# The gates of an RG-LRU in a fused decoder block: six 128-feature matmuls per step, or four by blocks of 64 features with the high and low parts stacked

## The chip, the cores and the metric

The kernel runs on one core of a Trainium2 chip. Its engines work side by side, each with its own instruction stream: TensorE (PE) multiplies matrices into PSUM, VectorE (DVE) and ScalarE (ACT) do elementwise work, GpSimd (POOL) does some as well, and DMAs, most of them issued by SyncE (SP), move data between HBM and the on-chip SBUF. The metric is the device time of one execution in microseconds. Before the change the median of three runs is 2132.93 us (2130.52 to 2132.96). The profiled execution took 2130.19 us, of which 2128.4 us lie between its first and its last instruction (the span).

## The reference

One layer of a decoder block over 2048 positions and 1024 features: a combined input projection to 9216 columns, a dilated-window attention branch, a gated linear recurrence (RG-LRU) branch, a merge, an output projection and a layer norm. The change concerns the recurrence's gates alone:

```python
def rg_lru(x, w_r, b_r, w_i, b_i, lam):
    xb = x.reshape(B, S, LRU_BLOCKS, LRU_BLOCK_WIDTH)          # 16 blocks of 64
    r = sigmoid(einsum('bsgi,gij->bsgj', xb, w_r).reshape(B, S, C) + b_r)
    i = sigmoid(einsum('bsgi,gij->bsgj', xb, w_i).reshape(B, S, C) + b_i)
    log_a = -LRU_C * r * softplus(-lam)
    a = exp(log_a)
    u = sqrt(maximum(-expm1(2.0 * log_a), 0.0)) * (i * x)
    # h_t = a_t * h_(t-1) + u_t, an associative scan over the positions
```

Here x is the output of a width-4 causal convolution. The gate weights are block-diagonal: a feature reaches only the 64 features of its own block.

## The kernel before

**Precision.** Every fp32 product is made from parts. A value is copied to a rounded type (fp32r) as its high part, and the rest, the value minus that, is its low part. A product of two such values takes three matmuls: high times high, high times low, low times high.

**Stages.** The projection comes first and takes until about 1453 us of the span. It computes 72 column tiles of 128 features over four chunks of 512 positions, by a Strassen-like scheme: two column tiles and two chunks at a time, seven products instead of eight. There are two halves (chunks 0 and 1, then 2 and 3) of 36 such units each, and each product has 12 matmuls of 128 rows by 512 columns into one of four PSUM banks (tag `q`). Attention follows, and then the merge, the output projection and the layer norm.

**Ticks and queues.** The program is put into order while it is built. A product is a tick, 506 of them (L902 to L920). In each tick come, in this order, the product's matmuls, the events fixed for this tick, the work put off with `later`, the chains, and the evacuation of the product's bank. Each engine's instructions run in the order of their emission, so an instruction that waits holds up all that stand behind it on its engine.

**Events** load and prepare the weights. `load_w` (L224) has SP load a block of weights (the tiles `wA` and `wS` of the profile), three to six ticks ahead of the unit's preparation. `sums` (L239) has DVE form the sums `S` of blocks, `prep_w` (L259) has ACT make the high part (`hA`, `hS`, L264) and DVE the low part (`l`). In the first half the low parts go to HBM (`wl_scr`), in the second half they are read back (`load_lo`, L279).

**Chains** are generators that work on from a finished tile. A chain asks (`Ask`) for free slots, a number of ticks to pass and a share of each engine's time in a tick (`LEN`, 2.75 us); what it asks for is taken from the tick's budget, and it goes on when budget, slots and conditions allow. `ALONE` scales DVE's share in the first half.

**The recurrence chain** `lru(i, c, ub)` (L427) handles feature tile i (128 features, two blocks) and chunk c, 32 chains in all; tiles 0, 2, 4 and 6 put chunk 1 off to the second half. In sixteen of them (`bring_gw`) the gate weights come first: two DMAs on SP into `gr` (L438, L439), each 128 rows of 128 numbers from the block-diagonal matrices that the layout built. Then follow the convolution into `v` (ACT L447, DVE L449), the high and the low part of the weights into `gw` (ACT L456, DVE), the high and the low part of v (`vh`, ACT L463; `vl`, DVE), the gate matmuls in the middle of the next product (L472 to L474, put there by `pe_later`), the two tanh that leave PSUM (ACT L485 for r, L486 for i, with the halved biases `brh`), the exponentials, the square root and the scan (L507). At most two such chains are live at a time, and `gate["busy"]` keeps one gate step at a time in the two PSUM banks of tag `g`.

**At the start** ACT issues the DMAs of the biases and the recurrence's vectors (L73, L78) before anything else; `consts` (L851) scales them once the first product has been emitted.

Of the kernel before, what the change touches and what calls it, by code (L numbers as in the profile page):

```python
# [8 lines left out]
F32 = mybir.dt.float32  # L9
F32R = mybir.dt.float32r  # L10
AF = mybir.ActivationFunctionType
ALU = mybir.AluOpType
# [19 lines left out]
def hybrid_block_kernel(ctx: ExitStack, tc: tile.TileContext, a: dict, out: bass.AP):  # L32
# [3 lines left out]
    def flat(t):  # L36
        return t.bitcast(F32)
# [39 lines left out]
    lr = cst.tile([P, 8, 8], F32, name="lr")  # L77
    act.dma_start(lr, a["lru_vec"])  # L78
    brh = cst.tile([P, 2, 8], F32, name="brh")
    sp2 = cst.tile([P, 8], F32, name="sp2")  # L80


# [47 lines left out]
    def take(name, dt=F32R):  # L130
        if not vacant:
            raise RuntimeError(f"no slot at {now['n']}: {[x[1].name if hasattr(x[1],'name') else x[1] for x in home.values()]} chains {len(chains)}")
        i = vacant.pop(0)
        t = sl_p.tile([P, CH], dt, tag=f"s{i}", name=name)
        home[id(t)] = (i, t)
        return t
# [81 lines left out]
    def tt(eng, out, in0, in1, op):  # L218
        eng.tensor_tensor(out=out, in0=in0, in1=in1, op=op)  # L219
# [207 lines left out]
    def lru(i, c, ub):  # L427
# [7 lines left out]
        if bring_gw:  # L435
            yield Ask(lag=0, need=1, keep=1)
            gr = take("gr" + nm, F32)
            sp.dma_start(gr[:, 0:P], a["wr"][i])  # L438
            sp.dma_start(gr[:, P:2 * P], a["wi"][i])  # L439
        if c == 1 and i in put_off:  # L440
            yield Ask(lag=4)
        yield Ask(lag=0, need=1, keep=6, cond=lambda: gate["live"] < 2 and begun[i] == c, ACT=1.3, DVE=2.7)
# [14 lines left out]
            tt(dve, w[:, 2 * P:], gr[:, 0:2 * P], flat(w[:, 0:2 * P]), ALU.subtract)  # L457
            give(gr)
        yield Ask(lag=0, cond=lambda: gated[i] == c)
        gw = GW[i].rearrange("p (l j f) -> p l j f", l=2, j=2)  # L460
        yield Ask(need=2, keep=1, ACT=.66, DVE=.75)
        vh, vl = take("vh" + nm), take("vl" + nm)
        act.activation(vh, v, AF.Copy)  # L463
        tt(dve, vl, v, flat(vh), ALU.subtract)
        yield Ask(lag=2, cond=lambda: not gate["busy"])
        gate["busy"] = True
        pg = []

        def gates():
            for j in range(2):  # L470
                g = ps.tile([P, CH], F32, tag="g", name=f"g{j}{nm}", bufs=2)
                pe.matmul(g, gw[:, 0, j], vh, start=True, stop=False)  # L472
                pe.matmul(g, gw[:, 0, j], vl, start=False, stop=False)
                pe.matmul(g, gw[:, 1, j], vh, start=False, stop=True)  # L474
                pg.append(g)
            give(vh, vl)
            if c in ((0, 3) if i in put_off else (1, 3)):
                give(GW[i])

        pe_later(1, gates)  # L480
        gated[i] = c + 1
        yield Ask(lag=2, need=3, keep=1, ACT=3.3, DVE=.75)
        gate["busy"] = False
        tr, ti, e = take("tr" + nm, F32), take("ti" + nm, F32), take("e" + nm, F32)
        act.activation(tr, pg[0], AF.Tanh, scale=0.5, bias=brh[:, 0, i:i + 1])  # L485
        act.activation(ti, pg[1], AF.Tanh, scale=0.5, bias=brh[:, 1, i:i + 1])  # L486
        act.activation(e, tr, AF.Exp, scale=sp2n[:, i:i + 1], bias=sp2n[:, i:i + 1])
        act.activation(e, e, AF.Identity, scale=0.5, bias=half_t)
        act.activation(tr, tr, AF.Tanh, scale=sp2[:, i:i + 1], bias=sp2[:, i:i + 1])
# [267 lines left out]
    at(base[len(seq)] - 10, drop_cs)  # L757
    at(base[len(seq)] + 12, lambda: load_cs(1))

    HALF = (slice(0, 64), slice(64, P))  # L760
    USLOT = (("X3", "X2"), ("X0", "X4"), ("Y0", "X1"))
    VSLOT = {(0, 0): "X5", (2, 0): "Y1", (1, 0): "Y2", (0, 1): "X5", (2, 1): "Y1", (1, 1): "Y2"}

# [87 lines left out]
    def consts():  # L851
        dve.tensor_scalar(out=bh, in0=b72, scalar1=0.5, scalar2=None, op0=ALU.mult)
        dve.tensor_scalar(out=bn, in0=b72, scalar1=-1.0, scalar2=None, op0=ALU.mult)
        dve.tensor_scalar(out=bq, in0=b72[:, 0:64], scalar1=0.25, scalar2=None, op0=ALU.mult)
        dve.tensor_scalar(out=brh, in0=lr[:, 5:7, :], scalar1=0.5, scalar2=None, op0=ALU.mult)
        dve.tensor_scalar(out=lrn, in0=lr[:, 0:4, :], scalar1=-1.0, scalar2=None, op0=ALU.mult)
        dve.memset(ubs, 0.0)
        dve.memset(hst, 0.0)
# [668 lines left out]
```

## Time and profile before

| | PE | DVE | ACT | POOL |
|---|---|---|---|---|
| busy in the span, us | 2093.8 | 1672.6 | 1078.8 | 457.6 |
| instructions | 12016 | 3193 | 2284 | 397 |

| | us |
|---|---|
| profiled execution | 2130.19 |
| its span | 2128.4 |
| median of three runs | 2132.93 |

The chain of work that ended last spends 37% of the span in the projection's matmuls (L602):

```profile
PE 60%; ACT 6%; DMA 3%; DVE 2%; issue 1%; SPq 1%; POOL 0%; DVEq 0%; ACTq 0%
```

The gate matmuls are 192 of the 12016, in three groups of 64 (L472, L473, L474). Weight loads onto the array are a row of their own (PEld) and overlap the matmuls. A matmul's record is longer than its share of PE, since matmuls are pipelined: the distance of starts is what one costs. In a row of the profile the bracket at the end says how long the engine stood idle before the instruction and what it waited for; SPq and ACTq are the queues that issue DMAs.

### The profile page before, as it was taken

Reading aid. Unit: us, or ns where it says so; the run is one execution under the profiler, and the core shown is the slowest. Engines: PE = TensorE matmul, PEld = TensorE weight load, DVE = VectorE, ACT = ScalarE, POOL = GpSimd, SP = SyncE. Lnnn points to the kernel's source line nnn. Section 1 sums busy time; section 2 is a strip of 40 time slices with the busy share of each in tenths; the row PEclk is TensorE's granted clock in tenths of the full one; section 3 lists DMA queues with packets and bytes.
Section 4 is the critical chain, followed back from the end, with each engine's and each line's share of the span. In section 5 each row is a group of like instructions: output and inputs, shape, how many; then the busy total and the mean of one; then the engine's idle time right before and its main releaser. Section 6 shows DMA issues by size and latency. Waiting matters only on the chain.

```text
span 2128.4 us, 35700 instructions
## 1 busy us (share of the span) xinstructions
PE 2093.8 (98%) x12016; PEld 1745.9 (82%) x12016; DVE 1672.6 (79%) x3193; ACT 1078.8 (51%) x2284; POOL 457.6 (22%) x397
## 2 busy tenths in 40 slices
PE   8999999999999999999999999999999999999998
PEld 7888888888878888888888888888888888878887
DVE  8888889799789867787787887886999645476667
ACT  6355445357356566546557656657999411121100
POOL 1001011011011002121221221223535444332120
PEclk9999999999999999999999999999999999999999
DMA  9987997988988876677778788879998688874431
GB/s 273 275 267 218 290 261 238 272 265 250 278 271 257 305 220 196 221 226 219 249 251 270 262 256 254 256 227 383 289 310 262 210 280 281 290 246 162 163 109 70
DMA packets 348263, 525.72 MB, mean 247 GB/s; under 512 B 123568, under 2 KB 156336, under 8 KB 344240
## 3 DMA queue, kind: packets, MB, share of 16 engines
q1 hardware_dynamic: 330368, 491.64, 71.3%
q0 software_dynamic: 10080, 18.35, 5.4%
q10 hardware_dynamic: 7632, 13.44, 1.7%
q8 instruction: 96, 1.57, 0.3%
q14 instruction: 87, 0.71, 0.1%
HBM read 318.18 MB, written 190.45 MB: 239 GB/s over the span
## 4 chain that ended last, share of the span: by engine, by line
PE 60%; ACT 6%; DMA 3%; DVE 2%; issue 1%; SPq 1%; POOL 0%; DVEq 0%; ACTq 0%
PE q L602 37%; ACT p L996 4%; PE z L1393 3%; PE z L1391 3%; PE z L1392 3%; PE yb L1281 2%; PE yb L1282 2%; PE yb L1283 2%; PE o L1034 1%; ACT ptb L1019 1%; PE ya L1361 1%; PE ya L1360 1%; PE ya L1359 1%; PE s L981 1%; DMA yb_scr<-gB 1%; DVE p L988 1%
## 5 line engine op out<-in xcount | busy, mean ns | idle before, releaser
L602 PE MATMUL q<-xT,hS 128*128 128x512 f32 x1680 | 518.8, 390 | 0.0
L602 PE MATMUL q<-xT,l 128*128 128x512 f32 x1120 | 436.0, 389 | 0.0
L602 PE MATMUL q<-xB,hA 128*128 128x512 f32 x1248 | 387.3, 392 | 5.7 <-ACT xB L207 5.7
L602 PEld LDWEIGHTS q<-xT,hS 128*128 128x128 f32 x1680 | 314.1, 188 | 64.3
L602 PE MATMUL q<-xB,l 128*128 128x512 f32 x904 | 352.9, 390 | 0.5 <-DMA l<-wl_scr 0.4
L602 PEld LDWEIGHTS q<-xB,hA 128*128 128x128 f32 x1248 | 234.1, 188 | 54.4 <-ACT xB L207 5.7
L602 PEld LDWEIGHTS q<-xT,l 128*128 128x128 f32 x1120 | 210.2, 188 | 44.3
L602 PEld LDWEIGHTS q<-xB,l 128*128 128x128 f32 x904 | 170.1, 188 | 37.5 <-DMA l<-wl_scr 0.8
L264 ACT ACTIVATE hA<-wA 128x512 fp32r<-128x512 f32 x218 | 135.5, 623 | 82.1 <-DMA wA<-in_w_in_dram 44.0
L602 PE MATMUL q<-xB,hS 128*128 128x512 f32 x560 | 173.5, 391 | 2.2 <-DVE v L219 2.2
L996 ACT ACTIVATE p<-p,sta 128x256 f32<-128x256 f32 (+1 forms) x384 | 172.2, 455 | 5.9 <-DVE sta L988 5.2
L602 PE MATMUL q<-xT,hA 128*128 128x512 f32 x560 | 172.8, 390 | 0.0
L237 POOL DMA_DIRECT2D wS<-in_w_in_dram x70 | 61.1, 935 | 477.6 <-DMA wS<-in_w_in_dram 120.0
L264 ACT ACTIVATE hS<-S 128x512 fp32r<-128x512 f32 x175 | 109.0, 623 | 87.9 <-DVE S L219 48.4
L219 POOL TENSOR_TENSOR S<-S,wA 128x512 f32<-128x512 f32 x35 | 45.6, 1303 | 445.8 <-DVE S L219 319.1
L602 PEld LDWEIGHTS q<-xB,hS 128*128 128x128 f32 x560 | 104.2, 188 | 23.8 <-issue 2.6
L602 PEld LDWEIGHTS q<-xT,hA 128*128 128x128 f32 x560 | 104.7, 188 | 21.9 <-issue 0.4
L988 DVE CUSTOM_DVE_ANT_0 p<-s,mask 128x256 f32<-128x256 f32 (+1 forms) x384 | 118.8, 360 | 4.6 <-PE s L981 3.6
L1393 PE MATMUL z<-wo,ml 128*128 128x512 f32 (+1 forms) x264 | 101.1, 383 | 0.8 <-DVE ml L1378 0.8
L1391 PE MATMUL z<-wo,mh 128*128 128x512 f32 (+1 forms) x264 | 101.1, 383 | 0.1
L1392 PE MATMUL z<-wo,mh 128*128 128x512 f32 (+1 forms) x264 | 101.0, 383 | 0.0
L1281 PE MATMUL yb<-h,wl 128*128 128x512 f32 x256 | 100.3, 392 | 0.0
(199 smaller groups left out, 4182.1 us busy)
## 6 DMA issues: line engine op xcount, KB each, us to landing
wA<-in_w_in_dram SPq DMA_DIRECT2D x253, 256.0 KB, 5.0
wl_scr<-l SPq DMA_DIRECT2D x105, 512.0 KB, 5.3
l<-wl_scr SPq DMA_DIRECT2D x105, 512.0 KB, 4.8
sw<-y SPq DMA_DIRECT2D x384, 64.0 KB, 3.1
wS<-in_w_in_dram SPq DMA_DIRECT2D x70, 256.0 KB, 4.8
wS<-in_w_in_dram POOLq DMA_DIRECT2D x70, 256.0 KB, 6.4
qh_scr<-hi SPq DMA_DIRECT2D x48, 256.0 KB, 5.8
v_scr<-vs SPq DMA_DIRECT2D x48, 256.0 KB, 4.4
```

The lines of the kernel that those rows point to most:

```text
L219: eng.tensor_tensor(out=out, in0=in0, in1=in1, op=op)
L237: pool.dma_start(t, w_part(s, x), accum_op=ALU.add)
L264: act.activation(h, r, AF.Copy)
L602: pe.matmul(bank, w[:, ks], x[:, kk, xx], start=(first and i == 0), stop=(last and i == 11))
L988: dve.tensor_tensor_reduce(out=st["p", i, j][:, h, lo:256], in0=st["s", i, j // 2][h][:, j % 2, lo:256], in1=mask[:, lo:256], scale=1.0, s ...
L996: act.activation(p, p, AF.Exp, scale=-1.0, bias=s[:, h:h + 1], accum_out=s[:, 2 + h:3 + h])
L1281: pe.matmul(yb, WL[f][:, 0, k], xx[:, 0], start=(k == 0), stop=False)
L1282: pe.matmul(yb, WL[f][:, 0, k], xx[:, 1], start=False, stop=False)
L1283: pe.matmul(yb, WL[f][:, 1, k], xx[:, 0], start=False, stop=(k == 7))
L1391: pe.matmul(z, mh[:, k], w[:, 0, hs], start=(k == 0), stop=False)
L1392: pe.matmul(z, mh[:, k], w[:, 1, hs], start=False, stop=False)
L1393: pe.matmul(z, ml[:, k], w[:, 0, hs], start=False, stop=(k == 7))
```

## The change

A tile of v has two blocks of 64 features. Before, both lie one above the other in the 128 rows, the weights hold zeros off the diagonal, and the high and the low part of v are two tiles of 128 rows. After, each block has a tile of its own, `vv[0]` and `vv[1]`, with the block's high part in one half of the rows and its low part in the other. The block's weights stand in both halves of the rows, the 64 columns of r beside the 64 columns of i, or the other way round for the second block. One matmul then multiplies the weights with the high and with the low part and adds them up, and gives both gates of the block. High and low parts of the weights make two matmuls for a block and four for a step, where there were six; the product low times low, which was left out, is now in.

To fill and empty these tiles, each operation between them and the full-height tiles is done once for each half of the rows: the copy and the subtraction that split v, and the tanh of r and of i. The subtraction of a half writes to the other half of the rows. The weights come by eight DMAs of 64 rows by 64 numbers, and the biases in the new order by four small DMAs on ACT's queue at the start. The chain asks for twice the time for the split, and between the tanh and the exponentials it now makes a new request, so that at least a tick passes there.

```diff
     brh = cst.tile([P, 2, 8], F32, name="brh")
+    HALF = (slice(0, 64), slice(64, P))
+    for hs, os in (HALF, HALF[::-1]):
+        act.dma_start(brh[hs, 0], a["lru_vec"][hs, 5])
+        act.dma_start(brh[hs, 1], a["lru_vec"][os, 6])
...
             gr = take("gr" + nm, F32)
-            sp.dma_start(gr[:, 0:P], a["wr"][i])
-            sp.dma_start(gr[:, P:2 * P], a["wi"][i])
+            for b, (hs, ns) in enumerate(((HALF[0], ("wr", "wi")), (HALF[1], ("wi", "wr")))):
+                for j in range(2):
+                    for rows in HALF:
+                        sp.dma_start(gr[rows, P * b + 64 * j:P * b + 64 * j + 64], a[ns[j]][i, hs, hs])
...
-        gw = GW[i].rearrange("p (l j f) -> p l j f", l=2, j=2)
-        yield Ask(need=2, keep=1, ACT=.66, DVE=.75)
-        vh, vl = take("vh" + nm), take("vl" + nm)
-        act.activation(vh, v, AF.Copy)
-        tt(dve, vl, v, flat(vh), ALU.subtract)
+        gw = GW[i].rearrange("p (l b f) -> p l b f", l=2, b=2)
+        yield Ask(need=2, keep=1, ACT=1.3, DVE=1.5)
+        vv = [take(f"vv{j}{nm}") for j in range(2)]
+        for x, hs, os in zip(vv, HALF, HALF[::-1]):
+            act.activation(x[hs], v[hs], AF.Copy)
+            tt(dve, x[os], v[hs], flat(x[hs]), ALU.subtract)
...
         def gates():
-            for j in range(2):
-                g = ps.tile([P, CH], F32, tag="g", name=f"g{j}{nm}", bufs=2)
-                pe.matmul(g, gw[:, 0, j], vh, start=True, stop=False)
-                pe.matmul(g, gw[:, 0, j], vl, start=False, stop=False)
-                pe.matmul(g, gw[:, 1, j], vh, start=False, stop=True)
-                pg.append(g)
-            give(vh, vl)
+            pg[:] = [ps.tile([P, CH], F32, tag="g", name=f"g{j}{nm}", bufs=2) for j in range(2)]
+            for b in range(2):
+                for l in range(2):
+                    pe.matmul(pg[b], gw[:, l, b], vv[b], start=(l == 0), stop=(l == 1))
+            give(*vv)
...
-        yield Ask(lag=2, need=3, keep=1, ACT=3.3, DVE=.75)
+        yield Ask(lag=2, need=2, keep=1, ACT=2.5)
         gate["busy"] = False
-        tr, ti, e = take("tr" + nm, F32), take("ti" + nm, F32), take("e" + nm, F32)
-        act.activation(tr, pg[0], AF.Tanh, scale=0.5, bias=brh[:, 0, i:i + 1])
-        act.activation(ti, pg[1], AF.Tanh, scale=0.5, bias=brh[:, 1, i:i + 1])
+        tr, ti = take("tr" + nm, F32), take("ti" + nm, F32)
+        for h, (hs, os) in enumerate((HALF, HALF[::-1])):
+            act.activation(tr[hs], pg[h][hs], AF.Tanh, scale=0.5, bias=brh[hs, 0, i:i + 1])
+            act.activation(ti[hs], pg[h][os], AF.Tanh, scale=0.5, bias=brh[os, 1, i:i + 1])
+        yield Ask(need=1, keep=1, ACT=2.0, DVE=.75)
+        e = take("e" + nm, F32)
...
-        dve.tensor_scalar(out=brh, in0=lr[:, 5:7, :], scalar1=0.5, scalar2=None, op0=ALU.mult)
+        dve.tensor_scalar(out=brh, in0=brh, scalar1=0.5, scalar2=None, op0=ALU.mult)
```

More of the change, by code (lines that the diff above doesn't have):

```diff
@@ L758, in hybrid_block_kernel @@
     at(base[len(seq)] + 12, lambda: load_cs(1))
-    HALF = (slice(0, 64), slice(64, P))
     USLOT = (("X3", "X2"), ("X0", "X4"), ("Y0", "X1"))
```

## The prediction

> **What bounds the kernel now.** I read the busy shares and the 40 slices first, then the busy times by stretch, then PE's own waits, then the gate instructions, and last the engines side by side around the loads of the gate weights.
>
> ```profile
> span 2128.4 us, 35700 instructions
> PE 2093.8 (98%) x12016; PEld 1745.9 (82%) x12016; DVE 1672.6 (79%) x3193; ACT 1078.8 (51%) x2284; POOL 457.6 (22%) x397
> PE   8999999999999999999999999999999999999998
> PEclk9999999999999999999999999999999999999999
> 400.00:750.00 350.00, 347.77 (x1533) 287.26 (x1532) 306.83 (x477) 191.08 (x314) 35.35 (x37) 1.00 0.87 270
> 1100.00:1453.00 353.00, 352.58 (x1559) 291.60 (x1559) 280.42 (x385) 216.92 (x349) 73.63 (x52) 1.00 0.81 261
> PE q L602 <- ACT xB L207: 5.7, 1, 5.7
> PE q L602 <- DVE v L219: 2.2, 1, 2.2
> PE q L602 <- DMA l<-wl_scr: 0.4, 1, 0.4
> ```
>
> A row of stretches has its length, then busy time of PE, PEld, DVE, ACT, POOL. TensorE is the bound: in the projection stage (to about 1453 us) it waits three times, 8.3 us in all, 5.7 of them before its first matmul. So a matmul taken out here shortens the run by its spacing, unless a new wait gives it back. DVE is the nearest other engine, 306.8 of 350 us in the second stretch quoted; ACT has 159 us free there.
>
> **The change, part by part.**
>
> *Matmuls, the gain.*
>
> ```profile
> L472 PE MATMUL g<-vh,gw 128*128 128x512 f32 x64 | 25.4, 397 | 0.0
> 111.57 0.39 PE L472 MATMUL g<-vh,gw 128*128 128x512 f32 x1
> 112.93 0.39 PE L602 MATMUL q<-xT,hS 128*128 128x512 f32 x1
> ```
>
> One of the 32 gate steps (8 feature tiles, 4 chunks) has six matmuls: the three lines L472 to L474, each x64. They start at 111.57 and the next product at 112.93, so each takes 1.36 / 6 = 0.227 us of PE although its record reads 0.39. The new step has four of the same form, 128 rows by 512 columns: 64 fewer, **-14.5 us**.
>
> *ACT and DVE instructions, added.*
>
> ```profile
> L463 ACT ACTIVATE vh<-v 128x512 fp32r<-128x512 f32 x32 | 19.8, 620 | 6.2 <-DVE v L449 4.4 <-DVE l L219 1.2 <-DVE y L548 0.6
> L219 DVE TENSOR_TENSOR vl<-v,vh x32: 675/684/1710, 103.8 to 1396.9; 128x512 fp32r<-128x512 f32 x32
> L485 ACT ACTIVATE tr<-g,brh 128x512 f32<-128x512 f32 x32 | 21.9, 685 | 10.1 <-PE g L474 9.6 <-PE g L473 0.3
> L602 PEld LDWEIGHTS q<-xB,hA 128*128 128x128 f32 x1248 | 234.1, 188 | 54.4 <-ACT xB L207 5.7 <-DVE xB L208 0.4 <-ACT hA L264 0.4
> ```
>
> Halving the rows leaves 512 elements per row. The trace has no ACT or DVE instruction on 64 of 128 rows with 512 elements, so one costs between half (time by elements) and all (time by elements of a row) of the full one; I take all: the rows quoted are the same operations with the same 512 elements per row, the nearest there are. Each step then adds one 0.62 us copy and two 0.685 us tanh on ACT (1.99 us, 64 us over 32 steps) and one 0.684 us subtraction on DVE (22 us in all). The work that hides them is PE's own stream: the weight conversions queued behind them on ACT (hA, hS) run so far ahead that PE's weight loads waited 0.4 us for them in the whole run. Without this cover the ACT part alone would cost 64 us. The one place where the DVE half is exposed is where PE already stands close behind it; that is counted below. The new pause in the chain (tr and ti first, e a tick later) moves work whose only reader is the scan, far from PE: nothing.
>
> *Six more loads per weight fetch, the price.* Sixteen times a chain fetches its gate weights (8 in each half), by two DMAs of 64 KB so far, by eight of 16 KB after. All are issued on SP, in order, ahead of the next stage's wA.
>
> ```profile
> L438 SPq DMA_DIRECT2D gr<-in_wr_dram x16: 372/424/1381, 86.8 to 1355.9; - x16
> 579.67 0.38 SPq L438 DMA_DIRECT2D gr<-in_wr_dram  x1
> 580.10 0.44 SPq L439 DMA_DIRECT2D gr<-in_wi_dram  x1
> 580.59 0.90 SPq L226 DMA_DIRECT2D wA<-in_w_in_dram  x2
> 584.07 0.42 ACT L456 ACTIVATE gw<-gr 128x256 fp32r<-128x256 f32 x1 [6.67 <-DMA gr<-in_wi_dram]
> 585.38 0.69 DVE L219 TENSOR_TENSOR S<-S,wA 128x512 f32<-128x512 f32 x1 [5.18 <-issue]
> 587.52 0.69 DVE L219 TENSOR_TENSOR vl<-v,vh 128x512 fp32r<-128x512 f32 x1
> 587.15 0.70 PE L602 MATMUL q<-xB,hS 128*128 128x512 f32 x2 [2.20 <-DVE v L219]
> 588.61 0.40 PE L472 MATMUL g<-vh,gw 128*128 128x512 f32 x1
> ```
>
> This is the only place where PE stalled for DVE. SP comes to gr late, ACT stands 6.67 us until it lands, and DVE stands 5.18 us until the wA issued right behind it is there (the row names no releaser; the same wait at 263 us below names wA). Then v, which frees a PSUM bank, and vl follow, and vl ends at 588.21, 0.40 before PE's gate matmul. The two gr issues start 0.43 us apart; six more put wA 6 x 0.43 = 2.6 us later. At the bounds: below 6 x 0.37 = 2.2 us (the row's minimum), above 6 x 0.9 = 5.4 us (between its median and its maximum, when the queue pushes back). A landing of fewer bytes could be quicker, but wA's size is unchanged and it is what ends DVE's wait. Two further fetches look the same, those of tiles 2 and 4:
>
> ```profile
> 263.02 0.69 DVE L219 TENSOR_TENSOR S<-S,wA 128x512 f32<-128x512 f32 x1 [5.35 <-DMA wA<-in_w_in_dram]
> 265.17 0.68 DVE L219 TENSOR_TENSOR vl<-v,vh 128x512 fp32r<-128x512 f32 x1
> 265.77 0.74 DVE L548 SCALAR_TENSOR_TENSOR y<-q,bn,v 128x512 f32<-128x512 f32 x1
> 267.65 0.48 PE L472 MATMUL g<-vh,gw 128*128 128x512 f32 x1
> 425.52 0.69 DVE L219 TENSOR_TENSOR S<-S,wA 128x512 f32<-128x512 f32 x1 [5.54 <-issue]
> 427.67 0.68 DVE L219 TENSOR_TENSOR vl<-v,vh 128x512 fp32r<-128x512 f32 x1
> 429.41 0.39 PE L472 MATMUL g<-vh,gw 128*128 128x512 f32 x1
> ```
>
> The room between the end of vl and PE's gate matmul is 1.80, 1.06 and 0.40 us. Each is asked for 2.6 + 0.68 (second half of the subtraction) = 3.3 us, so PE loses 1.5 + 2.2 + 2.9 = **+6.6 us**. Bounds: 5.4 us with the lower delay, 15.0 with the upper one; 0 if the planner puts these fetches elsewhere.
>
> The fetches of odd tiles leave wA more time:
>
> ```profile
> 635.95 1.01 SPq L226 DMA_DIRECT2D wA<-in_w_in_dram  x2
> 643.06 0.69 DVE L219 TENSOR_TENSOR S<-S,wA 128x512 f32<-128x512 f32 x1
> 1314.72 0.69 DVE L219 TENSOR_TENSOR vl<-v,vh 128x512 fp32r<-128x512 f32 x1 [0.59 <-POOL glg L219]
> 1320.24 0.39 PE L472 MATMUL g<-vh,gw 128*128 128x512 f32 x1
> ```
>
> Here 6.1 us pass from the end of wA's issue to its use, against 585.38 - 581.49 = 3.9 us where it is awaited; 2.6 us later it is 0.4 us late, 1.1 with the DVE half. Three such fetches cost between 0 and 3.3 us; I take **+0.7**, most of it being caught by the four PSUM banks. In the second half vl is ready 4.83 us ahead in the tightest step, quoted last, more than 3.3, and the wl_scr, wS and activation stores that also stand behind the loads on SP are awaited by engines that run ahead of PE: nothing. The POOL queue's accumulating DMA waits for wS, up to 2.6 us longer, for a stage that begins later.
>
> [...]
>
> [...] Rows of this case overlap: vl starts at 265.17 and lasts 0.68 us, its successor starts 0.60 us later. [...]
>
> *Four small loads at the start.*
>
> ```profile
> 1.25 0.45 ACTq L78 DMA_DIRECT2D lr<-in_lru_vec_dram  x1
> 1.73 1.28 ACT L264 ACT_TABLE_LOAD   x1 [1.73 <-PEq L1516]
> 4.14 0.63 ACT L264 ACTIVATE hA<-wA 128x512 fp32r<-128x512 f32 x1 [1.12 <-DMA wA<-in_w_in_dram]
> ```
>
> ACT's queue issues them before its table load: 4 x 0.45 = 1.8 us, of which 1.12 was idle; the first conversion and PE's first matmul come up to 0.7 us late. Bounds 0 (caught by later input waits) and 0.7; I take **+0.5**. The bias itself is read 100 us later.
>
> *Sum:* -14.5 + 6.6 + 0.7 + 0.5 = **-6.7 us**. The profiled execution took 2130.2 us (span 2128.4 and 1.8 around it), so 2123.5; the shown runs have their median 2.7 us above it, which gives **2126.2 us**.
>
> **Rivals.**
>
> 1. *All of it hidden.* The planner gives the loads or the chain another tick, or the small DMAs land in time. For it: 5 of 8 fetches in the first half and all in the second have room. Against: the three rows above, where SP is late already. -14.5 + 0.5: 2130.2 - 14.0 = 2116.2 to 2118.9 by the median.
> 2. *No change that shows.* SP's queue pushes back in the three fetches: their loss is 15.0, the odd ones' 0.7 to 3.3, sum +1.7 to +4.3 with the start; with 4 us per fetch they lose (4 + 0.68) x 3 - 3.26 = 10.8, sum -2.5. That is 2130.4 to 2134.6 or a little more, by the median. Against: at the place quoted gr's issues took 0.38 and 0.44.
> 3. *Slower.* One mechanism: SP's order ahead of wA. It decides from some 5.5 us of delay per fetch; the row's maximum, 1.38 us per issue, would give 8.3. At 6 us the three lose (6 + 0.68) x 3 - 3.26 = 16.8, and at three odd fetches wA comes 6 - 2.2 = 3.8 us late, of which I let PE feel half, 2 us each: sum 16.8 + 6 + 0.5 - 14.5 = +8.8, 2141.7. For it: one gr issue of 1.38 us was seen. Against: the median is 0.42.
> 4. *It doesn't do what it says:* four matmuls at a longer spacing, should the weight loads of two alternating blocks not hide. At 0.34 us they would cost the old 1.36 us and the sum be +7.8. Against: today's gate matmuls too change weights each time and keep 0.227.
>
> **How the numbers follow.** My forecast, a gain of 4.3 to 11 us, 0.49; rival 1, with the part between 11 and 14, 0.17; rival 2, 0.22; rivals 3 and 4 together 0.12, 3 holding most. About 0.2% (4.3 us) is what a measurement here tells from no change. Faster 0.66, same 0.22, slower 0.12. The range of 8 in 10 runs from rival 1 in the profiled execution's terms, 2116, to rival 2's upper end, 2134, leaving out rivals 3 and 4 and little else.
>
> **What would show it.** Steps right: g matmuls x128 in place of x192, 0.227 us apart; SP issuing wA some 2.6 us after its old distance from the first gr; DVE's waits for wA at the three places near 8 us; new PE waits, on vl or v, of 1.5 to 3 us there and none in the second half. Wrong: no new PE waits (rival 1), PE waits at odd tiles (rival 3), or PE waiting on ACT's tanh halves for a free gate bank, which I priced at nothing.

## The result and the profile after

The kernel with the change takes 2150.45 us, median of six runs (2147.07 to 2155.79), against 2131.72 (2128.34 to 2135.86) for the kernel before on the same chip: a ratio of 1.0096, 95% interval 1.0086 to 1.0107, so it is slower by some 20.5 us (the two medians are 18.7 apart) where the forecast had it 6.7 us faster. The profiled execution took 2147.07 us and is the fastest of the six: its mean granted clock is 0.994, that of the others 0.991 to 0.993.

The span and the busy times from the page of the changed kernel:

```profile
span 2145.4 us, 35881 instructions
PE 2087.3 (97%) x11952; PEld 1738.3 (81%) x11952; DVE 1701.6 (79%) x3225; ACT 1147.1 (53%) x2380; POOL 455.9 (21%) x397
```

PE's waits in its projection stage (engine, line, what it waited for: total us, times, longest):

```profile
PE q L610 <- DVE v L223: 18.1, 4, 7.3
PE q L610 <- ACT xB L211: 7.2, 1, 7.2
PE q L610 <- DMA l<-wl_scr: 6.0, 4, 2.6
PE g L480 <- ACT ti L492: 0.5, 1, 0.5
```

PE is still the bound, with 64 instructions fewer, but it stands more often. Its wait for v on DVE went from 2.2 us to 18.1, that for the low parts of the weights from 0.4 to 6.0, the first one (on ACT, for xB) from 5.7 to 7.2: 23.0 us of new waiting against 14.5 us of matmuls taken out. The wait for ti adds 0.5.

The groups of the changed instructions (count, then shortest, median and longest in ns):

```profile
L480 PE MATMUL g<-vv,gw x128: 387/389/775, 113.6 to 1418.7; 128*128 128x512 f32 x128
L491 ACT ACTIVATE tr<-g,brh x64: 666/684/687, 114.4 to 1424.9; 64x512 f32<-64x512 f32 x64
L223 DVE TENSOR_TENSOR vv<-v,vv x64: 684/687/692, 105.6 to 1412.1; 64x512 fp32r<-64x512 f32 x64
L445 SPq DMA_DIRECT2D gr<-in_wr_dram x64: 465/594/1702, 87.8 to 1379.6; - x64
```

128 gate matmuls are there in place of 192. An ACT or DVE instruction of these forms costs as much on 64 rows (medians 0.684 and 0.687 us) as on 128 in the kernel before (0.688 and 0.684), as I had taken it. A half load costs SP 0.594 us, not the 0.43 I had used.

The same place as in the prediction, tile 6 in the first half, as SP's queue, DVE and PE show it in the changed kernel (start, duration, instruction, in brackets the idle time before it):

```profile
588.40 3.81 SPq L340 DMA_DIRECT2D ql_scr<-rp  x1
592.31 3.58 SPq L329 DMA_DIRECT2D k_scr<-rp  x1
595.94 1.17 SPq L445 DMA_DIRECT2D gr<-in_wr_dram  x2
597.15 2.51 SPq L445 DMA_DIRECT2D gr<-in_wi_dram  x4
599.71 1.23 SPq L445 DMA_DIRECT2D gr<-in_wr_dram  x2
601.04 1.00 SPq L230 DMA_DIRECT2D wA<-in_w_in_dram  x2
...
605.34 0.69 DVE L223 TENSOR_TENSOR S<-S,wA 128x512 f32<-128x512 f32 x1 [9.20 <-issue]
...
607.59 1.40 DVE L223 TENSOR_TENSOR vv<-v,vv 64x512 fp32r<-64x512 f32 x2
609.03 0.69 DVE L223 TENSOR_TENSOR y<-q,v 128x512 f32<-128x512 f32 x1
...
607.11 1.19 PE L610 MATMUL q<-xB,hS 128*128 128x512 f32 x2 [7.32 <-DVE v L223]
608.10 0.63 PE L610 MATMUL q<-xB,l 128*128 128x512 f32 x1
```

wA is issued 5.10 us after the first gr; it was 0.92 (579.67 to 580.59). So the delay is 4.2 us, not 2.6, and DVE waits 9.2 us for it, not 5.2. The last two rows show something the sum has no term for: from 607.11 to 608.10 PE does two matmuls in 0.99 us, not 0.45. The windows of PE show the clock there (length, PE busy and instructions, granted clock, DMA share, GB/s):

```profile
607.11:610.70 3.59, 3.59 (x9) 0.50 0.76 283
611.35:614.94 3.59, 3.59 (x17) 1.00 1.03 240
```

Behind this wait of 7.32 us the granted clock is at 0.50 in the first window, which holds 9 matmuls where the second, at 1.00, holds 17. The same window behind the wait of 2.61 us for l at 1392.67 has 9 matmuls at 0.52.

The matmuls slowed by it lose 7.2 us in all, worked out below. So 23.0 + 0.5 + 7.2 - 14.5 = 16.2 us are accounted for, of the 19.8 by which the last matmul of the projection ends later (1474.8 against 1455.0). The other 3.6 are in many short stalls that were not followed, and the stages behind take 2.8 us less, for a reason not looked into.

### The profile page after: what moved, and what is told of

Read it like the earlier page. It is cut to its first block, busy times and chain, and to the rows that moved or that the text cites. A ratio compares the mean times of both kernels' runs of the same rounds, so it can differ in the third digit from the quotient of the medians.

```text
span 2145.4 us, 35881 instructions
## 1 busy us (share of the span) xinstructions
PE 2087.3 (97%) x11952; PEld 1738.3 (81%) x11952; DVE 1701.6 (79%) x3225; ACT 1147.1 (53%) x2380; POOL 455.9 (21%) x397
## 3 DMA queue, kind: packets, MB, share of 16 engines
q8 instruction: 95, 1.56, 0.3%
## 5 line engine op out<-in xcount | busy, mean ns | idle before, releaser
L610 PE MATMUL q<-xB,hS 128*128 128x512 f32 x560 | 177.9, 399 | 18.1 <-DVE v L223 18.1
L223 DVE TENSOR_TENSOR l<-wA,hA 128x512 fp32r<-128x512 f32 x113 | 79.4, 703 | 27.0 <-ACT hA L268 26.8
```

The source lines that it names most:

```text
L610: pe.matmul(bank, w[:, ks], x[:, kk, xx], start=(first and i == 0), stop=(last and i == 11))
```

## The experiments

The figures in us are the ratio less one, times the median of the kernel before, run beside it (2127 to 2130 us). The interval is some 2 us to either side for most, up to 4.7 for those with few runs.

### The change taken apart

**The changed kernel with one load per fetch.** The gate weights are stacked in HBM as the SBUF tile wants them, and one DMA brings all 128 rows of 256 numbers.

```diff
-            for b, (hs, ns) in enumerate(((HALF[0], ("wr", "wi")), (HALF[1], ("wi", "wr")))):
-                ...
+            sp.dma_start(gr[:, 0:2 * P], a["wg"][i])
```

> The changed kernel, with one load per weight fetch: the layout stacks each tile's weights to 128 rows of 256 numbers, so SP issues one DMA in place of eight. Theory (SP's order: six more loads ahead of wA and l are what costs): the PE waits on v at the three even tiles and the waits on l fall back to what the kernel before had (2.2 and 0.4 us) or less, the half clock in the projection is gone, and the gain of 64 matmuls shows: 11 to 14 us faster than the kernel before. Rival A (the halves on ACT and DVE put DVE behind) and rival B (the planner's new order does it): the waits stay, 10 to 17 us slower than before.

Measured: 2125.77 us, 0.9986 (0.9976 to 0.9995), -3.0 us, between the theory's -11 to -14 and the rivals' +10 to +17. The loads account for most of the loss. But PE still waits 2.7 us for v at tile 6, although SP has one issue fewer there than in the kernel before.

**The same, and the biases without their four loads.** The second order of the bias rows stands in the vector array that is loaded anyway.

```diff
-        act.dma_start(brh[hs, 0], a["lru_vec"][hs, 5])
-        act.dma_start(brh[hs, 1], a["lru_vec"][os, 6])
...
-        dve.tensor_scalar(out=brh, in0=brh, scalar1=0.5, scalar2=None, op0=ALU.mult)
+        dve.tensor_scalar(out=brh, in0=lr[:, 5:9:3, :], scalar1=0.5, scalar2=None, op0=ALU.mult)
```

> As the run before, and the second bias order comes with the other vectors in one DMA, so the four small loads at the start are gone. Every theory: PE's first matmul starts near 5.7 us again in place of 7.2, and the run is 1.5 us shorter than with them, too little for the timing alone; the trace decides.

Measured: 2124.78 us, 0.9979 (0.9970 to 0.9988), -4.5 us, 1.5 less than with them, as expected; the first matmul starts at 6.12. Four matmuls, and no added load: yet 10 us of the 14.5 are missing. PE's waits:

```profile
PE q L604 <- DVE v L220: 5.1, 3, 3.3
```

**The half loads alone**, in the kernel before.

```diff
-            sp.dma_start(gr[:, 0:P], a["wr"][i])
-            sp.dma_start(gr[:, P:2 * P], a["wi"][i])
+            for j, n in enumerate(("wr", "wi")):
+                for cols in (slice(0, 64), slice(64, P)):
+                    for rows in (slice(0, 64), slice(64, P)):
+                        sp.dma_start(gr[rows, P * j + cols.start:P * j + cols.stop], a[n][i, rows, cols])
```

> The kernel before, with its 128 x 256 weight tile fetched by eight DMAs of 64 rows by 64 numbers; nothing else changed, six matmuls and full-height operations. Theory: 20 to 28 us slower than before: three waits on v of 4 to 7 us in the first half, each with half clock after it, and waits on l in the second half of 4 to 7 us together. Rivals A and B: 0 to 4 us slower.

Measured: 2146.51 us, 1.0085 (1.0068 to 1.0102), +18.1 us, a little under the 20 to 28 expected and more than twice what I had put on loads and halves together.

```profile
589.20 3.43 SPq L441 DMA_DIRECT2D gr<-in_wr_dram  x4
592.68 2.52 SPq L441 DMA_DIRECT2D gr<-in_wi_dram  x4
595.24 1.06 SPq L226 DMA_DIRECT2D wA<-in_w_in_dram  x2
```

In these rows of SP's queue wA follows the first gr after 6.0 us. PE waits for v 12.7 us in all (6.1 the longest) and for l 1.9 us.

**The halves alone**: six matmuls and the loads as before; the split of v, the tanh and the requests to the planner as in the change.

```diff
-        act.activation(vh, v, AF.Copy)
-        tt(dve, vl, v, flat(vh), ALU.subtract)
+        for hs in HALF:
+            act.activation(vh[hs], v[hs], AF.Copy)
+            tt(dve, vl[hs], v[hs], flat(vh[hs]), ALU.subtract)
...
+        for hs in HALF:
+            act.activation(tr[hs], pg[0][hs], AF.Tanh, scale=0.5, bias=brh[hs, 0, i:i + 1])
+            act.activation(ti[hs], pg[1][hs], AF.Tanh, scale=0.5, bias=brh[hs, 1, i:i + 1])
```

> The kernel before, with the split of v and the two tanh done once for each half of the rows and the chain's requests as in the changed kernel; weights, loads and the six matmuls as before. Theory: 0 to 3 us slower (the DVE half is felt only where PE stands close behind). Rival A: 10 to 25 us slower. Rival B (the new requests reorder the work): 5 to 20 us slower too, with PE waits at other places than the fetches.

Measured: 2139.37 us, 1.0050 (1.0035 to 1.0065), +10.6 us. That is as much as is missing in the version above, and rival A's size.

**The four bias loads alone.**

```diff
+    for hs in (slice(0, 64), slice(64, P)):
+        act.dma_start(brh[hs, 0], a["lru_vec"][hs, 5])
+        act.dma_start(brh[hs, 1], a["lru_vec"][hs, 6])
```

> The kernel before with one edit: the two bias rows are loaded by four DMAs of 64 x 8 values on ACT's queue at the start, and the scaling reads that tile; the gates stay as they were. My term for the start said 0.5 us (bounds 0 and 0.7). The traces of the changed kernel say more: its first matmul started at 7.22 us against 5.66. Theory (the small loads hold up the queues at the start): first matmul 1 to 1.6 us later than in the kernel before, the run 1 to 2.5 us longer, no new wait of PE later. Rival (start and the rest are independent, later input waits catch it): run within 1 us of the kernel before.

Measured: 2131.55 us, 1.0014 (1.0004 to 1.0023), +3.0 us. The first matmul starts at 7.48, as expected. But a later wait grew too, which I had not expected: PE waits 2.64 us for v at tile 6 in place of 2.20, and half clock follows, from 592.33 to 595.74 us, where the kernel before has none. The parts sum to -14.5 (by the matmuls' spacing) + 18.1 + 10.6 + 3.0 = +17.2, and the whole measured +20.5.

**Eight loads of whole rows**: as many issues and bytes as the half loads, each 128 rows by 32 columns.

```diff
+            for j, n in enumerate(("wr", "wi")):
+                for q in range(4):
+                    sp.dma_start(gr[:, P * j + 32 * q:P * j + 32 * q + 32], a[n][i, :, 32 * q:32 * q + 32])
```

> The kernel before, with the gate weights fetched by eight DMAs of 128 rows x 32 columns instead of two of 128 x 128: as many issues as in the changed kernel and the same bytes each, but whole columns of rows. Tells whether the price per issue depends on the count alone or on the form. If an issue takes the 0.43 us of the 128-row loads of before, wA is issued 2.6 us later after the first gr than before, the waits at 265, 428 and 588 us sum to about 7 us more, and the run is 6 to 9 us longer. If it takes 0.6 us as the 64-row halves did, the delay is 4.2 us and the run 15 to 18 us longer, as in the run with the half loads alone. Small runs of 128 bytes that push back would make it more than 18.

Measured: 2138.79 us, 1.0042 (1.0027 to 1.0057), +8.9 us, half of what the half loads cost. SP's queue at tile 6:

```profile
586.17 1.82 SPq L440 DMA_DIRECT2D gr<-in_wr_dram  x4
588.03 2.95 SPq L440 DMA_DIRECT2D gr<-in_wi_dram  x4
591.02 0.91 SPq L226 DMA_DIRECT2D wA<-in_w_in_dram  x2
```

The first four take 0.46 us each here, the last four more; over all 128 the median is 0.430, where the half loads have 0.595. The time is at the upper end of the 6 to 9 us expected for issues of that price. So the form decides the price besides the count: issues on 64 rows were the dear ones.

### Why the halves cost anything

**The split alone**, the subtraction and copy by halves with their request.

```diff
-        yield Ask(need=2, keep=1, ACT=.66, DVE=.75)
+        yield Ask(need=2, keep=1, ACT=1.3, DVE=1.5)
...
+        for hs in HALF:
+            act.activation(vh[hs], v[hs], AF.Copy)
+            tt(dve, vl[hs], v[hs], flat(vh[hs]), ALU.subtract)
```

> The kernel before with v's copy and subtraction each done in two halves of 64 rows (32 more of each), six matmuls, loads and tanh as before. The run with both halvings was 10.6 us longer. Theory S (DVE's and SP's chain paces PE from 430 to 600 us, so DVE's 0.68 us per step is felt there): most of it, +5 to +9 us, with waits of PE for v near 430 and 592 us of 1.5 and 4 us and half clock behind the longer one. Rival T (the tanh halves hold the gate bank and ACT): 0 to +3 us. Rival R (the planner places the steps in another order for its changed costs): neither this run nor the one with the tanh halves reproduces it by itself.

Measured: 2129.70 us, 1.0004 (0.9994 to 1.0013): no difference that shows, and at tile 6 the first gr is issued at 580.06, against 579.67 in the kernel before. Theory S falls for the split by itself: 32 more subtractions on DVE alone cost nothing.

**The tanh alone**, by halves, with its changed request and pause.

```diff
+        yield Ask(lag=2, need=2, keep=1, ACT=2.5)
...
+        for hs in HALF:
+            act.activation(tr[hs], pg[0][hs], AF.Tanh, scale=0.5, bias=brh[hs, 0, i:i + 1])
+            act.activation(ti[hs], pg[1][hs], AF.Tanh, scale=0.5, bias=brh[hs, 1, i:i + 1])
+        yield Ask(need=1, keep=1, ACT=2.0, DVE=.75)
```

> The kernel before with each of the two tanh done in two halves of 64 rows (64 more instructions of about 0.68 us on ACT) and the pause after them, the split of v, matmuls and loads as before. Theory S (DVE's extra half is what costs): 0 to +3 us. Rival T (the tanh halves): +5 to +9 us with PE waits for a free gate bank (named by ti) or for xB. Rival R (the planner's order): anything, with waits at places where neither v nor ti is named.

Measured: 2133.08 us, 1.0016 (1.0005 to 1.0027), +3.4 us; PE waits for v 4.8 us in two places, none of them named by ti. The two parts give 4.3 us, together they cost 10.6: this is not a price per instruction.

**The requests alone**: no halves, only the planner's changed costs and pause.

```diff
-        yield Ask(need=2, keep=1, ACT=.66, DVE=.75)
+        yield Ask(need=2, keep=1, ACT=1.3, DVE=1.5)
...
-        yield Ask(lag=2, need=3, keep=1, ACT=3.3, DVE=.75)
+        yield Ask(lag=2, need=2, keep=1, ACT=2.5)
```

> The kernel before with nothing but the changed requests to the planner (ACT 1.3 and DVE 1.5 for the split; ACT 2.5 for the two tanh, then a pause with ACT 2.0 and DVE .75 ahead of e); every operation full height, every load as before. The split by halves alone was 0.7 us longer, the tanh by halves with their changed requests 4.0, both together 10.6. Rival R (the planner's new order is what costs: other instructions in front of the rope stores that SP issues ahead of the even tiles' gate weights): +4 us or more, with k_scr at tile 4 issued some 3 us later than in the kernel before (420.2) and PE waits near 430 and 592 us. Rival T (the extra ACT halves): within 1 us of the kernel before.

Measured: 2129.98 us, 1.0012 (1.0003 to 1.0021), +2.6 us: between the two theories, with k_scr at tile 4 issued at 418.7 against 416.8. So part of what the tanh with its requests cost (3.4) may be the requests.

**Both halves, the requests as before.**

```diff
-        yield Ask(need=2, keep=1, ACT=1.3, DVE=1.5)
+        yield Ask(need=2, keep=1, ACT=.66, DVE=.75)
```

> The kernel before with both halvings (split and tanh) but the requests to the planner as they were, and no pause after the tanh. Rival R (the order costs, not the operations): within 2 us of the kernel before, k_scr at tile 4 issued near 420 us, no PE wait over 2.7 us. Theory S or T (the added halves cost by their duration): +8 to +11 us as in the run with both halvings and the changed requests.

Measured: 2141.74 us, 1.0068 (1.0055 to 1.0081), +14.5 us, more than either theory had.

**Four matmuls, one load, second bias order, the requests as before.** The same edit as the last, in the version that took 0.9979.

```diff
-        yield Ask(lag=2, need=2, keep=1, ACT=2.5)
+        yield Ask(lag=2, need=3, keep=1, ACT=3.3, DVE=.75)
```

> Four matmuls, halves, the gate weights by one load and the second bias order in the existing load (the version that measured 0.9979 of before), now with the requests to the planner as they were before the change. If the order costs (rival R), 4 to 10 us less than that version's -4.5: -8 to -14 us against before, at most the 14.5 of the matmuls. If the halves cost by their duration, no difference from that version: -3 to -6 us.

Measured: 2133.66 us, 1.0027 (1.0018 to 1.0037), +5.7 us, 10 us worse than with the changed requests, where both theories had a gain. Both kernels refute rival R as the whole cause: with the halves in, the new requests help. In the kernel before they cost 2.6 us by themselves.

### Which wait it is

**wA earlier.** In the version that took 0.9979, the two weights whose arrival DVE awaits are issued six ticks ahead in place of three (the expectation calls the ticks units), in front of the rope's stores. Rope is the rotation of attention's q and k; DVE adds up its results (the tiles `rp`), and SP stores them to `qh_scr`, `ql_scr` and `k_scr`.

```diff
-for d, n in ((6, "S1"), (6, "S3"), (4, "A11"), (3, "A22"), (3, "A12")):
+for d, n in ((6, "S1"), (6, "S3"), (4, "A11"), (6, "A22"), (6, "A12")):
```

> The version with one load and the second bias order (0.9979 of before), the requests to the planner as in the change; the next stage's first weights (A22 and A12, the wA that DVE waits for) are issued in the first half six units ahead instead of three, so in front of the strided rope stores and the gate weights on SP. Theory (SP's order ahead of wA is what paces DVE and PE at tiles 2, 4 and 6): DVE's waits for wA of about 5 us go, and with them PE's 3.3 us at 589 us and its half clock: 3 to 7 us less than that version, -8 to -11 against before. Rival (DVE is itself the pace there, or v's own wait is next): within 2 us of that version. A further way to miss: wA's buffers are not free six units ahead, and SP stands there instead; then slower than that version.

Measured: 2123.75 us, 0.9984 (0.9976 to 0.9993), -3.4 us, no better. DVE at tile 6:

```profile
584.93 0.69 DVE L220 TENSOR_TENSOR S<-S,wA 128x512 f32<-128x512 f32 x1
589.45 0.42 DVE L220 TENSOR_TENSOR gw<-gr,gw 128x256 fp32r<-128x256 f32 x1 [3.83 <-ACT gw L456]
```

The wait for wA is gone, and the next instruction stands in its place: gw, whose load is still issued behind the rope's stores. So this run did not tell the theories apart. The next four put gr on ACT's queue as well, so that nothing DVE waits for there stands behind these stores.

**Four matmuls, neither load behind the stores.**

```diff
-            sp.dma_start(gr[:, 0:2 * P], a["wg"][i])
+            act.dma_start(gr[:, 0:2 * P], a["wg"][i])
```

> The version with one load per fetch, second bias order and early wA (0.9984 of before), with the gate weights' load moved from SP's queue to ACT's, so that neither wA nor gr stands behind the strided rope stores on SP. With the early wA alone DVE's waits for wA went, and 8.2 us of waits for gw took their place. Theory L (DVE runs without a gap at tiles 2, 4 and 6 except for the stalls on transfers that SP issues late, and these stalls are what PE feels): DVE's waits for wA and gw there under 2 us, PE waits for v under 2 us in all, -10 to -14 us against before. Rival D (DVE's own instructions pace PE there): PE waits for v of 3 to 6 us remain, -3 to -7.

Measured: 2115.29 us, 0.9936 (0.9924 to 0.9949), -13.6 us: nearly the whole of the 14.5, and the fastest kernel here. Theory L holds, rival D falls. PE's waits in the profiled execution, the slowest of the five (2118.87 us):

```profile
PE q L604 <- DMA l<-wl_scr: 1.6, 2, 0.8
PE q L604 <- DVE v L220: 1.1, 2, 0.9
```

**The halves, neither load behind the stores.** The edit of wA above and

```diff
-            sp.dma_start(gr[:, 0:P], a["wr"][i])
-            sp.dma_start(gr[:, P:2 * P], a["wi"][i])
+            act.dma_start(gr[:, 0:P], a["wr"][i])
+            act.dma_start(gr[:, P:2 * P], a["wi"][i])
```

> The kernel before with both halvings and the changed requests (10.6 us longer), with early wA and gr on ACT's queue. Theory L: the halves then cost little, 0 to +3 us against before. Rival D (the halves cost by DVE's own time): +7 to +11 us again.

Measured: 2127.41 us, 0.9988 (0.9979 to 0.9997), -2.6 us, a little better than the 0 to +3 expected. The 10.6 us are gone with the same work on DVE and ACT, and PE waits for v no more.

**The kernel before, neither load behind the stores**: the same two edits.

```diff
+            act.dma_start(gr[:, 0:P], a["wr"][i])
+            act.dma_start(gr[:, P:2 * P], a["wi"][i])
```

> The kernel before with nothing but early wA and gr on ACT's queue; the base of the other two. Its PE waits on DVE sum to 2.2 us, so -2 us at most by theory L and by rival D alike; more than +2 us would mean that the two loads cost elsewhere, and the other two runs are to be read against this one.

Measured: 2134.66 us, 1.0023 (1.0013 to 1.0033), +4.9 us: a miss for both. Its projection ends no later; the loss comes in the stage behind it, as this row of PE's waits shows:

```profile
PE s L981 <- DVE sta L988: 7.4, 1, 7.4
```

And its window there (length, then busy time of PE, PEld, DVE, ACT and POOL, granted clock, DMA share, GB/s):

```profile
1454.00:1480.00 26.00, 16.77 (x250) 15.49 (x251) 16.03 (x73) 17.55 (x65) 12.52 (x14) 0.80 1.03 405
```

The same window of the kernel before, in the same columns:

```profile
1455.00:1481.00 26.00, 23.28 (x365) 20.41 (x366) 21.09 (x98) 23.17 (x89) 11.97 (x14) 0.93 1.03 404
```

PE stands 7.4 us at the entry of the attention stage there, and the other two have no such wait. Why that order meets it was not tried. Against this base the kernel with the halves is 7.2 us shorter and the one with four matmuls 19.4, more than four matmuls can give, so this wait is in both differences. The two kernels without it are 12.1 us apart: that is what four matmuls (and one load in place of two) gave once the loads were out of the way.

**The changed kernel, its eight half loads on ACT's queue, wA early.**

```diff
-                        sp.dma_start(gr[rows, P * b + 64 * j:P * b + 64 * j + 64], a[ns[j]][i, hs, hs])
+                        act.dma_start(gr[rows, P * b + 64 * j:P * b + 64 * j + 64], a[ns[j]][i, hs, hs])
```

> The changed kernel as it is, eight half loads per fetch, with early wA and these loads on ACT's queue. Theory L: SP's 4.2 us of delay go, but ACT is held some 4.7 us by eight issues, which its conversions hide in part: -5 to +5 us against before, so 13 us or more less than the changed kernel. Rival D: +10 us or more against before, as the changed kernel, since DVE has the same work.

Measured: 2162.96 us, 1.0150 (1.0128 to 1.0172), +31.9 us. ACT's engine and queue at tile 6, from the timeline of this run:

```profile
598.58 3.96 ACTq L445 DMA_DIRECT2D gr<-in_wi_dram  x4
602.57 2.93 ACTq L445 DMA_DIRECT2D gr<-in_wr_dram  x2
605.55 0.63 ACT L268 ACTIVATE hA<-wA 128x512 fp32r<-128x512 f32 x1 [7.01 <-PE q L610]
```

PE's waits in its projection stage:

```profile
PE q L610 <- ACT e L633: 12.9, 4, 4.2
PE q L610 <- ACT hS L268: 8.5, 3, 4.0
PE q L610 <- DVE v L223: 0.8, 1, 0.8
```

ACT converts nothing for seven microseconds while it issues, and evicts no bank: the wait for v is down to 0.8 us, as theory L has it, and a new one for ACT takes its place. My expectation had ACT held 4.7 us, hidden in part; at tile 6 the eight issues take 8.1 us, they are not hidden, and the number is a miss. Eight issues are too many on either queue.

## Why the prediction was wrong, step by step

**The matmuls: right.** Four of them take 0.91 us of PE, 0.227 each, in the changed kernel too (start and duration):

```profile
113.59 1.07 PE L480 MATMUL g<-vv,gw 128*128 128x512 f32 x4
114.50 0.61 PE L610 MATMUL q<-xT,hS 128*128 128x512 f32 x2
```

Rival 4 is out. With the loads of the weights out from behind the stores, one for each fetch, the kernel gained 13.6 us of the 14.5.

**The three places: the step that failed most.** The sum had 6.6 us for tiles 2, 4 and 6. The new waits for v there are 4.60, 5.27 and 7.32 - 2.20 = 5.12, so 15.0. Three things went wrong in it.

*The price of a load* was too low. I took 0.43 us per half load, from two issues of 128 rows, and so a delay of 2.6 us with bounds of 2.2 and 5.4. It measured 4.1 to 4.2 us at each of the three. The form counts: the whole-row issues cost 8.9 us in all and the half rows 18.1. The mechanism, SP's order ahead of wA, was rival 3's, with 12 in 100 shared with rival 4. The price alone doesn't turn the sign: my own formula gives (4.2 + 0.68) x 3 - 3.26 = 11.4 us with it, and a sum of -1.9. What a half load costs shows in the runs: one load per fetch took the time from 1.0096 to 0.9986, and a load of 64 rows by 64 numbers held SP for 0.594 us where one of 128 rows by 128 held it for 0.424.

*The room was taken at the wrong instruction.* I measured from vl to the gate matmul. But PE waited for v, which DVE does ahead of vl, and without which the next product has no bank. The rows of the kernel before at tile 2:

```profile
263.97 0.68 DVE L219 TENSOR_TENSOR v<-u,q 128x512 f32<-128x512 f32 x1
265.93 0.62 PE L602 MATMUL q<-xB,hS 128*128 128x512 f32 x2
```

From v's end to that matmul it is 1.28 us, of which 0.15 pass even when PE waits (606.96 to 607.11 in the changed kernel). So the room is 1.1 us here, by the same rows 0.75 at tile 4 (427.15 to 428.05), and none at tile 6, where PE already stood 2.20 us for v. I had 1.80, 1.06 and 0.40. The second half of the step's own subtraction, which I added there, comes behind v and doesn't enter.

*The fetch itself came later*, which I had at nothing: against PE's products the first gr is issued 1.4, 1.8 and 1.4 us later than in the kernel before. At tile 2 the loads alone show most of it (1.1 us); at tiles 4 and 6 the halves alone do (2.3 and 2.1), the loads alone don't (-1.7 and -0.9). With the delays of wA, 12.4 us, these 4.6 and the rooms of 1.9 give 15.1, for the 15.0 measured.

**The clock: no term at all.** Behind the waits of 4.60, 5.27 and 7.32 us for v and of 2.61 us for l, the granted clock was at half for 3.41 or 6.83 us, part of it within the wait. A matmul takes 0.43 us then (608.10 to 608.53 in the row quoted and the next one), and the spacings in excess of 0.227 us behind these four waits sum to 7.2 us. Behind the wait of 1.75 us for l at 1155.95 it stayed at 1.00, and so it did in the kernel before behind the 2.20 us for v at 587.15. Over the projection stage of all the runs, the wait before the first matmul left aside, none of the waits from 1.4 to 1.83 us was followed by it, 7 of the 12 between 1.9 and 2.8 us were, and all of 3 us and more. So stalls of 1.5, 2.2 and 2.9 us were priced by their length alone, where waits about as long as the last two cost more in part of the cases. What decides that, and what sets the two lengths, no run shows.

**The halves at nothing: wrong, for a reason that bears on the loads too.** I looked for cover in PE's stream and found it, ACT's conversions being far ahead. But ahead of tiles 2, 4 and 6 PE's wait hangs on an order that goes round: DVE's rope sums, then SP's stores of them, one strided and slow (ql_scr, 4.34 us of issue at 571.54 in the kernel before), then gr and wA behind those on SP, then DVE again. A window ahead of DVE's stop at tile 6, of the kernel before (columns as above; DVE's is the third busy time):

```profile
559.00:580.10 21.10, 21.10 (x95) 17.48 (x94) 20.79 (x32) 8.36 (x16) 1.73 (x2) 1.00 1.00 250
```

The same window of the kernel with both halvings:

```profile
560.00:584.60 24.60, 24.60 (x109) 19.87 (x108) 23.30 (x36) 9.95 (x20) 1.76 (x2) 1.00 0.92 246
```

SP's queue and DVE of that kernel at the end of this window:

```profile
581.10 3.93 SPq L326 DMA_DIRECT2D k_scr<-rp  x1
585.09 0.43 SPq L439 DMA_DIRECT2D gr<-in_wr_dram  x1
586.11 0.85 SPq L227 DMA_DIRECT2D wA<-in_w_in_dram  x2
...
590.74 0.69 DVE L220 TENSOR_TENSOR S<-S,wA 128x512 f32<-128x512 f32 x1 [6.05 <-DMA wA<-in_w_in_dram]
```

DVE is busy 95 to 99% of the time up to the point where it stops for wA; what delays its rope sums also delays the stores, and with them the loads that it will wait for. The first gr comes at 585.09 in place of 579.67. PE has 1.1 us of room or less there, so what is above that is felt, and the clock's step comes on top. That the loop is what costs, and not the work, is shown by the two runs that open it: with the same halves, the loss of 10.6 us became a gain of 2.6, and the four matmuls' gain went from 4.5 to 13.6. DVE is no less busy in the second of them (31.31 of 32 us from 560 to 592 us).

What it is in the halves that makes the sums late is not shown. The first gr at tiles 4 and 6 is issued at 420.33 and 579.67 us in the kernel before, at 420.27 and 580.06 with the split alone, 423.14 and 580.38 with the requests alone, 423.67 and 582.43 with the tanh and its requests, 423.53 and 585.09 with all of it, 423.74 and 588.17 with both halves and the old requests. The split's added work on DVE did not move it by more than 0.4 us; the order of the instructions and the work on ACT have a part that no run separates.

On the size of the subtraction's halves, the quoted rows show the two halves of vv from 607.59 to the next start at 609.03, 1.44 us where two whole subtractions take 1.20 (0.60 from a whole vl to its successor, in the prediction's rows). So each half took 0.12 us more from start to start than a whole one, though these rows show no wait of DVE there. What causes it no run separates.

**The second half at nothing: wrong.** I named the stores behind the loads on SP and overlooked the loads of low parts that PE itself reads. SP's queue and PE near 1380 us in the changed kernel:

```profile
1378.93 1.23 SPq L445 DMA_DIRECT2D gr<-in_wr_dram  x2
1380.26 0.53 SPq L286 DMA_DIRECT2D l<-wl_scr  x1
...
1384.42 1.52 SPq L286 DMA_DIRECT2D l<-wl_scr  x2
...
1392.67 0.70 PE L610 MATMUL q<-xB,l 128*128 128x512 f32 x1 [2.61 <-DMA l<-wl_scr]
```

The load issued at 1380.26, right behind gr, landed at 1384.28 and ended a wait of 1.05 us. The longest wait, quoted last, ended with the first of the two issued at 1384.42, which stand behind wA and more stores and took 8.2 us to land, where the median of these loads is 4.8. Waits for l grew by 5.6 us in all, but only from 0.4 to 1.9 with the half loads alone: part of it hangs on the order of the whole, and which part was not separated.

**The start: under-sized.** I took 0.5 us, four issues at 0.45; it measured 3.0. ACT's queue in the changed kernel:

```profile
1.73 0.53 ACTq L82 DMA_DIRECT2D brh<-in_lru_vec_dram  x1
4.73 1.28 ACT L268 ACT_TABLE_LOAD   x1 [4.73 <-DMA wA<-in_w_in_dram]
```

The table load comes 3.0 us later (4.73 against 1.73), and SP's four loads of x beside them take 4.29 in place of 1.84 us. The first matmul starts 1.56 us later (7.22 against 5.66). In the kernels with these four loads it starts at 7.22 to 7.59 us, in all others at 5.66 to 6.90. With the four loads alone the traces hold the rest as well: 1.8 us at the start, 0.4 more of waiting at tile 6 and 1.6 lost to the half clock behind it make the 3.8 us between the two profiled executions (2134.01 and 2130.19). So in that execution most of what the four loads cost beyond the start was the clock's step, at a place far from it.

**The odd tiles: right in size, by luck.** Of the four waits for v in the changed kernel the fourth, 0.9 us at 542 us, is the only one away from tiles 2, 4 and 6; I had put 0.7. But I had put it down to a late wA, and the wait that DVE has ahead of it (2.31 us at 528.90) is for ACT's hS. PE's wait on the halved ti, which I had named as a sign of error, comes once, 0.5 us.

## What to carry to other kernels

Where an engine stops for a transfer, follow that transfer's queue back to what stands ahead of it, and that to who produces it: if it is the engine that stops, the two pace each other, and a delay can come back as a later load, whatever cover the engines' shares promise. Then a cheap move, here two loads out from behind a slow store, can be worth more than the work saved. Take the room at the instruction that the bound engine waits for, and not at the one that you change. Price a DMA by a row of its own form and not by its count (here 0.594 us against 0.424 for an issue), and allow for the clock behind a stall that comes near 2 us, where these runs had half clock behind some of the waits.

## What the runs showed of the hardware

- DMA issues on 64 rows by 64 numbers held SP 0.594 us (median of 64 for each array), those of 128 rows by 128 numbers, with four times the bytes, 0.424 (median of the 16 for r) and 0.444 (for i).
- Half clock (granted 0.50) came behind waits of PE as short as 1.96 us (the changed kernel with its loads on ACT), and did not come behind one of 2.74 us (four matmuls, one load, the requests as before); in the changed kernel it lasted 3.41 or 6.83 us.
- ACT's tanh and DVE's subtraction took the same time for 64 rows of 512, 0.684 and 0.687 us, as for 128, 0.688 and 0.684.
- k_scr, stored in plain rows, held SP for 3.58 us at tile 6, right behind the strided ql_scr with its 3.81 us; at 1374.74 us, with SP idle before it, 0.32.
